# ScalarE copies the high parts of the exponentials, the state space outputs come one stage later, and the softmax sums are asked for later

## The chip, the cores and the metric

The kernel runs on one core of a Trainium2 chip. The metric is the device time of one execution in microseconds (us). The core has five engines with a queue of instructions each: TensorE (PE in the profile; PEld is its weight load), VectorE (DVE), ScalarE (ACT), GpSimd (POOL) and SyncE (SP). The first four compute, and SP issues the DMAs. An instruction waits at the head of its queue until the semaphores that it names are reached, and everything behind it on that engine waits with it.

## The reference

One layer of a decoder trunk, sequence 1024, width 1024, in fp32: three causal mixers side by side (forgetting attention, an S5 state space, HGRN2), merged by gates, then cross attention and SwiGLU. The change touches the first two mixers.

```python
def fox_attention(q, k, v, log_f):        # 8 heads x 64
    c = jnp.cumsum(log_f, axis=1)
    ...
        s = jnp.einsum('bqhd,bkhd->bhqk', qi, k, preferred_element_type=jnp.float32) * scale
        s = s + ci[..., None] - c_keys
        s = jnp.where(k_pos[None, :] <= q_pos[:, None], s, -jnp.inf)
        p = jax.nn.softmax(s, axis=-1).astype(v.dtype)
        return jnp.einsum('bhqk,bkhd->bqhd', p, v)

def s5_mixer(u, a_re, a_im, b_re, b_im, c_re, c_im, d_skip, log_dt, w_glu, b_glu):   # 32 groups x 16
    ...
    _, _, h_r, h_i = lax.associative_scan(_complex_linear_combine, elems, axis=1)
    y = (jnp.einsum('bsgp,ghp->bsgh', h_r, c_re.astype(f32))
         - jnp.einsum('bsgp,ghp->bsgh', h_i, c_im.astype(f32)))
    y = y.reshape(bsz, seq, S5_W) + d_skip.astype(f32) * uf
    z = jax.nn.gelu(y)
    out = z * jax.nn.sigmoid(z @ w_glu.astype(f32) + b_glu.astype(f32))
    return out.astype(u.dtype)

def reference(x, mem, ...):
    h = rmsnorm(x, norm_mix[l])
    proj = h @ w_in[l]
    ...
    merged = (gates[:, :, 0] * (y_fox @ wb[:BRANCH_W])
              + gates[:, :, 1] * (y_s5 @ wb[BRANCH_W:2 * BRANCH_W])
              + gates[:, :, 2] * (y_hg @ wb[2 * BRANCH_W:]))
    x = x + merged @ w_out[l]
    x = x + cross_attention(rmsnorm(x, norm_x[l]), rmsnorm(mem, norm_mem[l]), ...)
    x = x + swiglu(rmsnorm(x, norm_ffn[l]), w_gate_up[l], w_down[l])
```

## The kernel before

An fp32 product is made of three matmuls. Every operand is split into a high part (a rounded copy) and a low part (the operand minus that copy), and high by high, low by high and high by low are accumulated in PSUM. So each weight and each activation passes through a copy and a subtraction before TensorE may use it. Matmuls are at most 128 x 512, one PSUM bank.

The program is written as generators that are mixed while it is recorded. `drive` steps the generator of the current stage, and `pump` puts pieces of the input projection between its steps. These fillers (tiles `pj`, from a fixed list of jobs) are counted by an account of TensorE time, `self.pe`. `later(us, fn)` asks for a piece of work at the first step at which that account has moved on by `us`. `ahead(n, fn)` records a piece with a higher priority, by n places: 60 for the state space stage, 60 for the splitting of weights, 20 for what `later` asked for, 10 for the attention. A scheduler then orders each engine's instructions by priority and by data dependences, which follow the order in which the code was recorded. Big tiles live in an arena of 50 slots; a slot is reused when its last reader is done.

**The state space stage** (`s5_main`, some 115 to 320 us of the span) treats 32 groups of channels in 8 blocks of four groups, o = 0 to 7. Each block passes four stages, one block behind the other:

- `s5_prep(o)`: 8 DMAs on SP (L1095) load the block's inputs into a tile `s5u`, and GpSimd makes the block's matrices `s5x`.
- `s5_prep2(o)`: VectorE makes the rotations `s5e`; TensorE makes `s5g` and `s5k`; ScalarE copies both out of PSUM; 8 DMAs on SP (L1163) lay the copy of `s5k` out as a block Toeplitz matrix `toep`.
- `s5_body(o)`: TensorE makes `s5d1`; VectorE multiplies it into `s5dd`, runs the scan, and makes the carried states `kcs`.
- `s5_out(o)`: TensorE makes `s5y` out of `toep` with the inputs and out of `kcs`, alternately for the four groups. VectorE and ScalarE apply the gelu in `s5u`, and 8 DMAs on SP (L1218) store it to `sz_d`.

There are two buffers of `toep` and two of `kcs`, taken in turn:

```python
self.toep, self.kcs = ([t[:, 512 * i:512 * i + 512].rearrange("p (g c) -> p g c", g=4) for i in range(2)]
...
tz = self.toep[o % 2]                                     # in s5_prep2(o)
for s in range(8):
    nc.sync.dma_start(out=tz[16 * s:16 * s + 16, :, 16 * s:128], in_=ktv[:, :, 0:128 - 16 * s])
...
self.mm(c, tz[:, g], U[:, g], True, False)                # in s5_out(o): reads toep, then kcs
self.mm(c, Z1[:, g].rearrange("p k h -> p (k h)"), kc[:, g], False, True)
```

**The attention stage** (`fox_main`, some 320 to 640 us) has 16 units, one for each head and each half of the queries. A unit steps over 4 or 8 blocks of 128 keys. At each, TensorE makes scores `st`, ScalarE their exponentials `pf`, and GpSimd copies these to the high part of `pt` (a 128 x 512 block, on the diagonal 384, 256 and 128 wide ones). VectorE subtracts for the low part, GpSimd adds `pf` into the running sum `facc`, and TensorE multiplies `pt` by the values two blocks later (`pv`). Between them stand the maxima of the next unit: TensorE makes `mx`, VectorE reduces it to `mc`, TensorE transposes that (`mt`). At a unit's end `fox_out` splits `facc` into `ah`, high part on ScalarE and low part on VectorE. After every second unit it asks by `later` for `sums`: four matmuls `sm` with `ah`.

The buffer number that ends a name in the orders below tells tiles apart. The inputs `s5u` of blocks 0 to 7 are 868, 932, 1052, 1183, 1376, 1598, 1784 and 1983.

Of the kernel before, what the change touches and what calls it, by code (L numbers as in the profile page):

```python
# [13 lines left out]
AF = mybir.ActivationFunctionType  # L14
ALU = mybir.AluOpType
# [32 lines left out]
S5_US = 4.5  # L48
S5_W = (1.0, 0.6, 1.0, 1.2)
FOX_AT = 8  # L50
S5_END = 1.5
S5_BEG = 1.75
AH_P = 0
# [134 lines left out]
class Trunk:  # L188
# [538 lines left out]
                out.append(piece(i, c))  # L727
        return out + [chain, rows]

    hi_pool = (0, 1, 2, 3)  # L730

    def fox_main(self):
        units = self.fox_units()
        pend = deque()
        pre = self.fox_pre(units[0])
        for i, f in enumerate(pre):
            f()
            yield FOX_P[i >= len(pre) - 3]

        def drain(n):  # L740
            while len(pend) > n:
                pend.popleft()()

        for ui, un in enumerate(units):
            p, half, h = un
            self.unit = ui
            pre = self.fox_pre(units[ui + 1]) if ui + 1 < len(units) else []
            nj = 4 * half + 4
            per = [[] for _ in range(nj)]
            if pre:  # L750
                body, tail = pre[:-2], pre[-2:]
                w = nj - PRE_END[half]
                per[0].append(body.pop(0))
                b = BUILD[half]
                for i, f in enumerate(body):
                    per[min(b + i * (w - b) // len(body), w - 1)].append(f)
                per[w - 1].append(tail[0])
                per[nj - 1].append(tail[1])
            acc = self.u("facc")[:, 0:512]
            st = {}  # L760
            pf = None
            for j in range(nj):
                q0 = max(0, 128 * j - 512 * half)
                ps = self.psm("st")
                diag = j >= 4 * half
                self.mm(ps[:, q0:512], self.k1[h][:, 128 * j:128 * j + 128], self.q1[h][:, q0:512], True, False)
                self.mm(ps[:, q0:512], self.k2[h][:, 128 * j:128 * j + 128], self.q2[h][:, q0:512], False, not diag)
                if diag:
                    self.mm(ps[:, q0:q0 + 128], self.ident_r, self.mkq_r, False, True)
                if j % 2 == 0:  # L770
                    pf = self.u("pf").rearrange("p (a b) -> p a b", a=2)
                pr = pf[:, j % 2, q0:512]
                self.act(pr, ps[:, q0:512], AF.Exp)
                pt = self.u("pt", F32R).rearrange("p (a b) -> p a b", a=2)
                if j % 4 in self.hi_pool:
                    self.ts(pt[:, 0, q0:512], pr, 1.0, 0.0, ALU.mult, ALU.add, self.nc.gpsimd)
                else:
                    self.act(pt[:, 0, q0:512], pr, AF.Copy)
                self.sub(pt[:, 1, q0:512], pr, pt.bitcast(F32)[:, 0, q0:512])
                if j == 0:  # L780
                    p0 = pr
                elif j == 1:
                    self.add(acc[:, q0:512], p0[:, q0:512], pr, self.nc.gpsimd)
                    if q0:
                        self.ts(acc[:, 0:q0], p0[:, 0:q0], 1.0, eng=self.nc.vector)
                else:
                    self.add(acc[:, q0:512], acc[:, q0:512], pr, self.nc.gpsimd)

                def pv(j=j, q0=q0, pt=pt, un=un, st=st, nj=nj, acc=acc):
                    p, half, h = un  # L790
                    if j == 0:
                        st["o"] = self.psm("pv")
                    for i in range(2):
                        self.mm(st["o"][:, q0:512], self.vst[j][:, 256 * p + 128 * h:256 * p + 128 * h + 128], pt[:, i, q0:512],
                                start=j == 0 and i == 0, stop=j == nj - 1 and i == 1)
                    if j == nj - 1:
                        self.fox_out(un, st["o"], acc)
                pend.append(pv)
                drain(PV_LAG)
                for f in per[j]:  # L800
                    f()
                yield (0.5 + 0.5 * (512 - q0) / 512) * HALF_W[half] * (FOX_E[j - nj] if j >= nj - 2 else 1.0)
        while pend:
            yield 0.5
            drain(len(pend) - 1)
        yield

    def fox_out(self, un, o, acc):
        p, half, h = un
        b = 64 * h  # L810
        s, so = slice(b, b + 64), slice(64 - b, 128 - b)
        hs = slice(512 * half, 512 * half + 512)
        hd = 2 * p + h
        if half == 0 and h == 0:
            self.fy[p] = self.u(f"fy{p}")
        t = self.u("ft")
        self.act(t[s, 0:512], o[so], AF.Copy)
        self.add(self.fy[p][s, hs], o[s], t[s, 0:512])
        ah = self.u("ah", F32R).rearrange("p (a b) -> p a b", a=2)
        self.split(acc, ah[:, 0], ah[:, 1])  # L820

        self.fah.append((hd, ah))

        def sums():
            ps = self.psm("sm")
            todo, self.fah = self.fah, []
            for n, (hd_, a_) in enumerate(todo):
                for i in range(2):
                    self.mm(ps[0:8], self.ohc_r[:, hd_, 0:8], a_[:, i], start=n + i == 0,
                            stop=n == len(todo) - 1 and i == 1)  # L830
            if p == 0:
                self.nc.vector.tensor_copy(out=self.fsum[0:8, hs], in_=ps[0:8])
            else:
                self.add(self.fsum[0:8, hs], self.fsum[0:8, hs], ps[0:8])
        if h == 1:
            self.later(2.0, sums)
        if half == 1 and h == 1:
            self.nc.sync.dma_start(out=self.fy_d[p], in_=self.fy[p])

# [381 lines left out]
    def s5_main(self):  # L1221

        self.s5o = {}
        for o in range(11):
            for lag, stage in ((0, self.s5_prep), (3, self.s5_out), (1, self.s5_prep2), (2, self.s5_body)):
                if 0 <= o - lag < 8:
                    stage(o - lag)
                    yield S5_W[lag] * (S5_END if o > 8 else S5_BEG if o < 2 else 1.0)
            if o == FOX_AT:
                self.need("ff")  # L1230
                self.fox_alloc()
# [958 lines left out]
```

## Time and profile before

| | us |
|---|---|
| median of three runs | 2177.76 |
| the three runs | 2176.45, 2177.76, 2184.1 |
| the profiled execution, its own time | 2179.96 |
| its span in the trace | 2177.9 |
| PE busy in the span | 2105.1 |
| DVE, ACT, POOL busy | 1438.1, 775.3, 437.0 |

The profiled execution's time is 2.2 us above the median, and its span covers all but 2.1 us of it. Times in the trace count from the span's start. A wait of an engine is its idle time just before an instruction, put down to the event that came last. A matmul's duration overlaps that of the next one, so the time that a row of matmuls takes is read from the distance of their starts.

### The profile page before, as it was taken

Reading aid. Unit: us, or ns where it says so; the run is one execution under the profiler, and the core shown is the slowest. Engines: PE = TensorE matmul, PEld = TensorE weight load, DVE = VectorE, ACT = ScalarE, POOL = GpSimd, SP = SyncE. Lnnn points to the kernel's source line nnn. Section 1 sums busy time; section 2 is a strip of 40 time slices with the busy share of each in tenths; the row PEclk is TensorE's granted clock in tenths of the full one; section 3 lists DMA queues with packets and bytes.
Section 4 is the critical chain, followed back from the end, with each engine's and each line's share of the span. In section 5 each row is a group of like instructions: output and inputs, shape, how many; then the busy total and the mean of one; then the engine's idle time right before and its main releaser. Section 6 shows DMA issues by size and latency. Waiting matters only on the chain.

```text
span 2177.9 us, 26388 instructions
## 1 busy us (share of the span) xinstructions
PE 2105.1 (97%) x10176; PEld 1728.0 (79%) x10176; DVE 1438.1 (66%) x2193; ACT 775.3 (36%) x1208; POOL 437.0 (20%) x399
## 2 busy tenths in 40 slices
PE   7998999999999999999999999998899999999999
PEld 5887776677788888888888888786688888878887
DVE  8887898889745566537665677665877777753421
ACT  4113255555421322227244455433433333331210
POOL 4271204454531111002411000011211111100000
PEclk9999999999999999999999999999999999999999
DMA  4432220111211011125434434142222222172311
GB/s 162 138 99 71 51 84 20 49 48 31 68 63 41 28 68 54 64 107 194 154 107 154 147 107 145 65 154 92 87 87 81 74 78 87 68 277 79 122 55 57
DMA packets 74925, 202.40 MB, mean 93 GB/s; under 512 B 13352, under 2 KB 23080, under 8 KB 74800
## 3 DMA queue, kind: packets, MB, share of 16 engines
q1 hardware_dynamic: 74800, 200.72, 26.7%
q8 instruction: 80, 1.31, 0.2%
q14 instruction: 45, 0.37, 0.1%
HBM read 156.51 MB, written 42.99 MB: 92 GB/s over the span
## 4 chain that ended last, share of the span: by engine, by line
PE 67%; DVE 3%; ACT 1%; issue 1%; DMA 1%; POOL 0%; SPq 0%; POOLq 0%; DVEq 0%; ACTq 0%
PE pj L221 43%; PE fp L221 18%; PE hs L221 2%; PE xo L221 1%; PE rs L221 1%; PE xs L221 1%; PE ho L221 1%; PE hst L221 0%; DVE xr L251 0%; DMA xr<-x_d 0%; PE pv L221 0%; POOL t L239 0%; PE st L221 0%; PE fb L221 0%; DVE wl L239 0%
## 5 line engine op out<-in xcount | busy, mean ns | idle before, releaser
L221 PE MATMUL pj<-xh,wh 128*128 128x512 f32 x784 | 312.2, 403 | 7.2 <-ACT xh L236 5.8
L221 PE MATMUL pj<-xl,wh 128*128 128x512 f32 x784 | 314.1, 404 | 4.8 <-DVE xl L251 4.8
L221 PE MATMUL pj<-xh,wl 128*128 128x512 f32 x784 | 310.2, 399 | 0.0
L239 DVE TENSOR_TENSOR wl<-wr,wh 128x1024 fp32r<-128x1024 f32 (+3 forms) x162 | 193.2, 1194 | 51.0 <-ACT wh L236 49.0
L221 PE MATMUL fp<-th,wc 128*128 128x512 f32 x640 | 206.8, 389 | 0.0
L236 ACT ACTIVATE wh<-wr 128x1024 fp32r<-128x1024 f32 (+3 forms) x162 | 155.0, 960 | 144.2 <-PE pj L221 58.0
L221 PE MATMUL fp<-fx,wc 128*128 128x512 f32 x720 | 175.0, 392 | 7.5 <-ACT wc L236 7.3
L221 PEld LDWEIGHTS pj<-xh,wh 128*128 128x128 f32 x784 | 148.4, 189 | 39.8 <-ACT xh L236 6.3
L239 DVE TENSOR_TENSOR xr<-pj,xr 128x512 f32<-128x512 f32 x80 | 54.8, 689 | 186.5 <-PE pj L221 177.2
L221 PEld LDWEIGHTS pj<-xl,wh 128*128 128x128 f32 x784 | 147.9, 189 | 36.7 <-DVE xl L251 7.1
L221 PEld LDWEIGHTS pj<-xh,wl 128*128 128x128 f32 x784 | 148.3, 189 | 30.6 <-issue 2.2
L221 PEld LDWEIGHTS fp<-fx,wc 128*128 128x128 f32 x720 | 136.1, 189 | 36.8 <-ACT wc L236 7.8
L221 PEld LDWEIGHTS fp<-th,wc 128*128 128x128 f32 x640 | 120.1, 188 | 25.0
L221 PE MATMUL pj<-hh,wh 128*128 128x512 f32 x352 | 133.9, 391 | 3.0 <-ACT hh L236 3.0
L221 PE MATMUL pj<-hh,wl 128*128 128x512 f32 x352 | 133.9, 391 | 1.4 <-DVE wl L239 1.4
L221 PE MATMUL pj<-hl,wh 128*128 128x512 f32 x352 | 134.2, 392 | 0.5 <-DVE hl L239 0.5
L221 PE MATMUL fp<-tl,wc 128*128 128x512 f32 x320 | 124.5, 389 | 0.0
L239 POOL TENSOR_TENSOR fc<-fc,fs 128x512 f32<-128x512 f32 x40 | 58.2, 1454 | 327.6 <-ACT fs L236 317.7
L239 DVE TENSOR_TENSOR pt<-pf,pt 128x512 fp32r<-128x512 f32 (+1 forms) x96 | 94.4, 985 | 40.1 <-POOL pt L255 39.8
L239 POOL TENSOR_TENSOR acc<-acc,sq 128x512 f32<-128x512 f32 (+1 forms) x18 | 30.7, 1707 | 375.4 <-ACT sq L236 375.3
L255 POOL TENSOR_SCALAR pt<-pf 128x512 fp32r<-128x512 f32 (+1 forms) x96 | 67.6, 705 | 139.1 <-ACT pf L236 127.8
L236 ACT ACTIVATE fs<-fc 128x512 f32<-128x512 f32 x40 | 25.3, 632 | 154.7 <-DVE fc L239 154.7
(415 smaller groups left out, 4758.9 us busy)
## 6 DMA issues: line engine op xcount, KB each, us to landing
wr<-w_in SPq DMA_DIRECT2D x48, 512.0 KB, 4.2
wr<-w_gu SPq DMA_DIRECT2D x44, 512.0 KB, 3.8
h_d<-fc SPq DMA_DIRECT2D x22, 512.0 KB, 2.6
hr<-h_d SPq DMA_DIRECT2D x22, 512.0 KB, 6.0
gz_d<-gz SPq DMA_DIRECT2D x20, 512.0 KB, 2.9
gate<-gz_d SPq DMA_DIRECT2D x20, 512.0 KB, 3.4
wr<-xo SPq DMA_DIRECT2D x17, 512.0 KB, 4.9
xr<-x_d SPq DMA_DIRECT2D x16, 512.0 KB, 6.2
```

Source lines behind the costliest of these rows:

```text
L221: self.nc.tensor.matmul(out, lhsT, rhs, start=start, stop=stop)
L236: self.nc.scalar.activation(out=out, in_=in_, func=f, **kw)
L239: return (eng or self.nc.vector).tensor_tensor(out=out, in0=a, in1=b, op=op)
L255: (eng or self.nc.vector).tensor_scalar(out=out, in0=a, scalar1=s1, scalar2=s2, op0=op0, **kw)
```

## The change

Three edits:

- in `fox_main` the high part of all 96 blocks of `pt` is copied by ScalarE (an ACTIVATE with Copy) in place of GpSimd;
- in `s5_main` the stages of one round o are recorded as prep(o), prep2(o-1), out(o-3), body(o-2); before, out(o-3) stood ahead of prep2(o-1);
- in `fox_out` the sums are asked for 6.0 us of TensorE's account later, in place of 2.0.

```diff
+SUM_AT = 6.0
...
-    hi_pool = (0, 1, 2, 3)
...
-                if j % 4 in self.hi_pool:
-                    self.ts(pt[:, 0, q0:512], pr, 1.0, 0.0, ALU.mult, ALU.add, self.nc.gpsimd)
-                else:
-                    self.act(pt[:, 0, q0:512], pr, AF.Copy)
+                self.act(pt[:, 0, q0:512], pr, AF.Copy)
                 self.sub(pt[:, 1, q0:512], pr, pt.bitcast(F32)[:, 0, q0:512])
...
         if h == 1:
-            self.later(2.0, sums)
+            self.later(SUM_AT, sums)
...
         for o in range(11):
-            for lag, stage in ((0, self.s5_prep), (3, self.s5_out), (1, self.s5_prep2), (2, self.s5_body)):
+            for lag, stage in ((0, self.s5_prep), (1, self.s5_prep2), (3, self.s5_out), (2, self.s5_body)):
```

Blocks b and b+2 share a buffer of `toep`. With the new order of the code, the copies of block b+2 into that buffer are recorded ahead of the reads of block b, for b = 0 to 5. So these six blocks read the matrix of the block two further on, which changes this part of the computation, and their first read depends on the eight copies of block b+2. The buffers of `kcs` are not crossed in this way.

What moves is shown at three places. The line numbers of the changed kernel are one higher in the helpers and four lower in the state space code.

**TensorE at the output of block 1.** `s5y` with `s5u_932` is block 1's output, `s5g` and `s5k` with `s5x_1192` are block 3's matrices, `s5d1_1545` belongs to block 2, and `pj` are filler matmuls. Before:

```order
L221 MATMUL pj_1412<-xh0_78,wh_1256 128x512
L221 MATMUL s5y_1419<-s5u_932,toep_823 128x128
L221 MATMUL pj_1412<-xl0_86,wh_1256 128x512
...
L221 MATMUL s5y_1419<-kcs_824,s5x_941 128x128
...
L221 MATMUL pj_1476<-wh_1365,xh0_78 128x512
L226 MATMUL s5g_1503<-cst_76,s5x_1192 128x128 x4
L221 MATMUL s5k_1508<-s5cx_643,s5x_1192 16x16
L221 MATMUL s5k_1508<-s5x_1192 16x112
...
L221 MATMUL s5d1_1545<-s5u_1052,s5x_1061 128x128 x4
```

After:

```order
L227 MATMUL s5g_1427<-cst_76,s5x_1192 128x128 x4
L222 MATMUL s5k_1432<-s5cx_643,s5x_1192 16x16
L222 MATMUL s5k_1432<-s5x_1192 16x112
...
L222 MATMUL pj_1412<-xl0_86,wh_1262 128x512
...
L222 MATMUL pj_1412<-xh7_85,wl_1263 128x512
L222 MATMUL s5y_1463<-s5u_932,toep_823 128x128
L222 MATMUL s5y_1463<-kcs_824,s5x_941 128x128
...
L222 MATMUL s5d1_1545<-s5u_1052,s5x_1061 128x128 x4
```

Block 3's matrices moved ahead of block 1's output; between the last `s5k` and the first `s5y` stand 23 filler matmuls.

**SP around the copies of blocks 5 and 6.** `toep_823<-s5u_1598` are the copies of block 5 (the last of the eight stands here), `toep_823<-s5u_1784` those of block 6. `sz_d` with `s5u_1183` and `s5u_1376` are the stores of blocks 3 and 4; `s5u_1983` are the loads of block 7; `wr` is a raw weight. Before:

```order
L1218 DMA sz_d_72<-s5u_1183 16x4x128 x8
L1163 DMA toep_823<-s5u_1598 16x512
...
L1163 DMA toep_823<-s5u_1598 16x4x16
L341 DMA wr_1970<-w_in 128x1024
L1095 DMA s5u_1983<-su_d_69 16x4x128 x8
L341 DMA wr_2074<-w_in 128x1024
L1163 DMA toep_823<-s5u_1784 16x512
L1218 DMA sz_d_72<-s5u_1376 16x4x128 x8
```

After:

```order
L1159 DMA toep_823<-s5u_1598 16x512
...
L1159 DMA toep_823<-s5u_1598 16x4x16
L1214 DMA sz_d_72<-s5u_1183 16x4x128 x8
L342 DMA wr_1970<-w_in 128x1024
L1091 DMA s5u_1983<-su_d_69 16x4x128 x8
L1159 DMA toep_823<-s5u_1784 16x512
L1159 DMA toep_823<-s5u_1784 16x4x112
```

The stores of an output moved behind the copies of the block two further on, and the copies of block 6 still stand behind the loads of block 7.

**TensorE at the sums after a pair of units, in the middle of the attention.** `sm` are the sums with two units' `ah`, `pv_4301` is the last output of the unit that ends there, `st_4405` and (after) `st_4411`, `pv_4391`, `mx` belong to the next. Before:

```order
L221 MATMUL pv_4301<-pt_4331,vs_1754 128x128
L221 MATMUL pj_4284<-xh5_83,wh_3996 128x512
...
L221 MATMUL pj_4284<-xh7_85,wl_3997 128x512
L221 MATMUL pj_4392<-xh0_78,wh_3996 128x512
L221 MATMUL sm_4399<-ah_4252,crr_170 8x512 x2
L221 MATMUL sm_4399<-ah_4379,crr_170 8x512
L221 MATMUL st_4405<-q12a_2350,k10_2346 128x512
```

After:

```order
L222 MATMUL st_4411<-q12a_2344,k10_2340 128x512
...
L222 MATMUL pv_4391<-pt_4364,vs_1619 128x512
...
L222 MATMUL mx_4424<-k21_2343,qmm_2346 128x128
L222 MATMUL mx_4424<-crr_170 128x128
L222 MATMUL mx_4428<-k21_2343,qmm_2346 128x512
L222 MATMUL sm_4431<-ah_4246,crr_170 8x512 x2
L222 MATMUL sm_4431<-ah_4373,crr_170 8x512 x2
L222 MATMUL st_4443<-q12a_2344,k10_2340 128x512
```

The sums moved behind a block of the next unit's scores, outputs and maxima.

## Rows read from the trace of the kernel before

**Rows 1.** The page's first part: busy time of each engine in us, its share of the span, and its instructions.

```profile
PE 2105.1 (97%) x10176; PEld 1728.0 (79%) x10176; DVE 1438.1 (66%) x2193; ACT 775.3 (36%) x1208; POOL 437.0 (20%) x399
```

**Rows 2.** Windows of 50 us, one in the state space stage and one in the attention: start and end; length; busy time of PE, PEld, DVE, ACT and POOL with their instructions; granted clock of TensorE, share of the DMA engines, GB/s.

```profile
200.00:250.00 50.00, 45.93 (x222) 38.02 (x220) 41.36 (x75) 12.03 (x24) 11.75 (x10) 0.93 0.16 38
500.00:550.00 50.00, 45.96 (x207) 35.53 (x206) 44.83 (x64) 26.78 (x45) 26.01 (x30) 0.97 0.07 22
```

**Rows 3.** Waits of TensorE from 150 to 620 us: engine, tile and line that waited, what released it; us in total, times, the longest.

```profile
PE s5y L221 <- DVE kcs L239: 10.1, 6, 3.3
PE sm L221 <- DVE ah L239: 8.0, 5, 2.3
PE mt L226 <- DVE mc L239: 7.9, 9, 1.7
PE pj L221 <- DVE wl L239: 1.5, 2, 0.9
PE st L221 <- ACT q12a L236: 1.4, 3, 0.6
...
PE sm L221 <- ACT ah L236: 0.4, 1, 0.4
```

**Rows 4.** The same windows as in group 2, 4 us long, around two waits of the state space stage and one of the attention.

```profile
168.00:172.00 4.00, 2.72 (x12) 2.72 (x13) 1.79 (x3) 0.00 (x0) 0.00 (x0) 0.65 0.42 156
172.00:176.00 4.00, 4.00 (x19) 3.37 (x19) 2.24 (x6) 0.95 (x2) 0.00 (x0) 0.92 0.00 0
...
208.00:212.00 4.00, 4.00 (x17) 3.81 (x17) 2.33 (x8) 0.00 (x0) 0.00 (x0) 0.50 0.03 5
212.00:216.00 4.00, 4.00 (x15) 3.16 (x15) 4.00 (x8) 2.55 (x3) 0.00 (x0) 0.80 0.16 31
...
512.00:516.00 4.00, 3.14 (x10) 2.51 (x11) 2.63 (x5) 1.12 (x2) 1.24 (x2) 0.74 0.00 0
516.00:520.00 4.00, 4.00 (x17) 3.31 (x17) 3.53 (x5) 1.03 (x2) 2.49 (x3) 0.83 0.41 110
```

**Rows 5.** Timeline of TensorE at these waits and at the places that the change moves: start, duration, engine, line, operation, tile and shape, number of instructions, idle time before the first and its releaser.

```profile
169.28 0.80 PE L221 MATMUL s5y<-kcs,s5x 128*128 128x128 f32 x2 [2.61 <-DVE kcs L239]
...
207.67 0.80 PE L221 MATMUL s5y<-kcs,s5x 128*128 128x128 f32 x2 [3.33 <-DVE kcs L239]
...
213.94 0.40 PE L221 MATMUL pj<-wh,xl 128*128 128x512 f32 x1
214.17 0.40 PE L221 MATMUL pj<-wl,xh 128*128 128x512 f32 x1
...
234.55 1.05 PE L221 MATMUL s5d<-s5u,s5x 128*128 128x128 f32 x8
...
256.57 0.35 PE L221 MATMUL s5k<-s5x 128*16 128x112 f32 x2
...
356.29 0.40 PE L221 MATMUL sm<-ah,crr 128*8 128x512 f32 x1 [1.78 <-DVE ah L239]
...
512.86 0.40 PE L221 MATMUL sm<-ah,crr 128*8 128x512 f32 x1 [2.29 <-DVE ah L239]
```

**Rows 6.** Timeline of ScalarE: the copy that follows that `s5k`.

```profile
257.60 0.57 ACT L236 ACTIVATE s5u<-s5k 16x512 f32<-16x512 f32 x1
```

**Rows 7.** Timeline of SP's queue: eight issues each of the `toep` copies, of the stores of an output and of the loads of a block, with the time from the first to the end of the last.

```profile
181.35 5.05 SPq L1163 DMA_DIRECT2D toep<-s5u  x8
...
217.96 3.59 SPq L1218 DMA_DIRECT2D sz_d<-s5u  x8
224.55 4.80 SPq L1095 DMA_DIRECT2D s5u<-su_d  x8
```

**Rows 8.** The view of one tile, `toep`: from issue to landing.

```profile
DMA to landing us min/median/max: 1.7/1.9/2.7
```

**Rows 9.** Timeline of VectorE: the work around block 1's and block 2's outputs (`z` is a filler's evacuation, `negc` ends a chain of the forget gates, `wl` is a weight's low part, `s5u` the gelu), and the end of block 4's body.

```profile
177.08 0.69 DVE L239 TENSOR_TENSOR z<-pj,Rb 128x512 f32<-128x512 f32 x1
...
184.88 2.29 DVE L531 TENSOR_TENSOR_SCAN negc<-on,a 128x1024 f32<-128x1024 f32 x1
187.88 1.23 DVE L239 TENSOR_TENSOR wl<-wr,wh 128x1024 fp32r<-128x1024 f32 x1 [0.72 <-ACT wh L236]
...
211.06 1.12 DVE L251 SCALAR_TENSOR_TENSOR s5u<-s5u,s5rv,s5y 128x128 f32<-128x128 f32 x4 [1.67 <-PE s5y L221]
...
217.25 0.68 DVE L239 TENSOR_TENSOR s5u<-s5u 128x512 f32<-128x512 f32 x1
...
246.45 1.38 DVE L239 TENSOR_TENSOR s5dd<-s5dd,s5e 64x508 f32<-64x508 f32 x2
```

**Rows 10.** Groups of instructions from 330 to 620 us by line, engine, operation, tile and shape: count; busy time, mean ns of one; idle time of the engine before them and what ended it.

```profile
L239 DVE TENSOR_TENSOR pt<-pf,pt 128x512 fp32r<-128x512 f32 x47 | 61.0, 1301 | 30.7 <-POOL pt L255 30.5
L255 POOL TENSOR_SCALAR pt<-pf 128x512 fp32r<-128x512 f32 x47 | 34.8, 744 | 62.7 <-ACT pf L236 56.9 <-DVE pt L239 2.3 <-DVE ah L239 2.2
L239 POOL TENSOR_TENSOR facc<-facc,pf 128x512 f32<-128x512 f32 x24 | 34.7, 1446 | 4.6 <-ACT pf L236 4.6
L236 ACT ACTIVATE pf<-st 128x512 f32<-128x512 f32 x47 | 27.8, 597 | 48.5 <-PE st L221 40.0 <-DVE pt L239 6.0 <-DVE fy L239 1.4
...
L239 DVE TENSOR_TENSOR ah<-facc,ah 128x512 fp32r<-128x512 f32 x15 | 11.1, 742 | 0.2
L236 ACT ACTIVATE ah<-facc 128x512 fp32r<-128x512 f32 x15 | 9.4, 625 | 0.6 <-DVE pt L239 0.5
```

## The prediction

> **What bounds the kernel now.** I read the page's first part, then windows over the two stages that the change touches, then TensorE's waits there, and last the timelines around the longest of them. TensorE is busy 97% of the span [rows 1], so only its idle time and its slow clock can be won or lost here; its work stays the same. From 150 to 620 us it waits for few things [rows 3]: `s5y` for `kcs` 10.1 us, `sm` for `ah` 8.0 and 0.4, `mt` for `mc` 7.9, a weight's low part 1.5, ScalarE's `q12a` 1.4. In all of them but the last and the 0.4 VectorE is late. It is busy 41.4 of 50 us in the state space stage and 44.8 of 50 in the attention, where ScalarE has 26.8 and GpSimd 26.0 [rows 2].
>
> A long wait costs a second time. After the waits of 2.61 and 3.33 us at 169.28 and 207.67, and after that of 2.29 at 512.86 [rows 5], the mean granted clock of the next windows is 0.65 and 0.92, 0.50 and 0.80, 0.74 and 0.83 [rows 4]: matmuls ran partly at 1.2 GHz. The loss is one minus the clock, times 4 us: 1.7, 2.8 and 1.7 us. The wait of 1.78 at 356.29 is followed by matmuls 0.40 long and close together, so I count no loss there.
>
> **Part 1, the outputs one stage later.** What it removes: all of the 10.1 us, if VectorE has finished `kcs` by the later place, and with it 1.7 + 2.8 us of clock. With the 1.5 for weights, which lies on the same chains, the stage now loses 16.1 us.
>
> What it adds is a dependence. The first `s5y` matmul of block b now waits for the eight copies of block b+2 into the same `toep` buffer, and those come late by their nature: they begin with block b+2's `s5k`, which now stands right ahead of it. From the end of `s5k` (256.57 + 0.35) to the end of ScalarE's copy (257.60 + 0.57) it is 1.25 us [rows 5, 6]. Eight issues take 5.05 us of SP's queue, the last starting some 4.4 us in [rows 7], and a copy lands 1.9 us after issue [rows 8]: 7.55 us. The cover is filler matmuls, 0.23 us apart [rows 5]. By the order after, 23 of them, 5.3 us, stand in it for blocks 1, 2, 4 and 5, and about 10.6 us for blocks 0 and 3. So four waits of at least 2.3 us follow, 9.2 us, each as long as one that lost clock before. Behind the waiting `s5y` on TensorE stand fillers, the next block's `s5d1` and the next `s5g`; VectorE's gelu and the slot of the inputs wait in turn.
>
> What SP has in front of the copies comes on top. Block 1: the copies of block 3 stand behind eight stores and four of the eight loads that came free late; I estimate 3.5 us. Block 2: the copies of block 4 stand behind the stores of block 1's output and the loads of block 6. That output's gelu runs on VectorE after the forget gates' chain. From 177.77 (end of `z`) to 187.17 (end of `negc`) it is 9.4 us, then two weight parts of 1.2, the evacuation 1.1, some 6 us of work in between (from 211.06 to 217.93 before it is 6.9 with the evacuation) [rows 9], eight stores 3.6 and eight loads 4.8 [rows 7], and copies and landing 6.3: 33 us. TensorE has 90 matmul rows, 20.4 us, between the outputs of blocks 1 and 2. That is a loss of 12.5 us with the clock after block 1, or 6.5 if the 6 us in between is overlapped; I take 9. Block 4: the loads of block 7 wait for a slot until block 4's body is done. From its `s5d1` at 234.55 [rows 5] to the end of `s5dd` at 247.83 [rows 9] it is 13.3 us, with 2.9 of block 3's gelu put ahead 16.2; then loads 4.6 and copies 6.3: 27 us against 18.5 of TensorE's rows, a loss of 8.5. Block 5: 1 us, since the copies of block 7 start while TensorE stands at block 4. Left of the waits for `kcs`, at the last two blocks, 2 us. Slow clock after blocks 2 and 4 as after 207.67, 2.8 each.
>
> Sum: 3.5 + 9 + 2.8 + 8.5 + 2.8 + 1 + 2 = 29.6, against 16.1: **+13 us**. Low end: every wait at its floor of 2.3 us, no clock lost, 2 us for `kcs`: 11.2 - 16.1 = -5. High end: 12.5 in place of 9, and blocks 0 and 3 waiting 2.3 each: 37.7 - 16.1 = +21.
>
> **Part 2, the sums later.** The four matmuls of a sum wait for the low part of `ah`, 8.4 us over six waits, the longest 2.29 [rows 3, 5]. By the order, 2.2 to 3.9 us of matmul time stood between a unit's last `pv` and the last `sm` matmul; now 5.5 to 11.3. Needed is at most 3.9 + 2.3 = 6.2, so the waits go nearly all, and the 1.7 us of clock after 512.86 with them: **-10**. What is late next is `mt`, since VectorE is as busy as before. The sums hold a PSUM buffer no longer than before, and the tile `ah` some 4 us longer.
>
> **Part 3, the copies on ScalarE.** GpSimd loses 96 copies, 47 of the wide ones 744 ns each [rows 10]. ScalarE gains them, 128x512 fp32r out of fp32 in SBUF, the same form as `ah<-facc` on ScalarE, 625 ns [rows 10]: 48 x 0.625 = 30 us for the wide ones, and between 0 and 30 for the narrower ones; I estimate 18 by their widths. That is 48 us in some 320 us of attention, about 7.5 in 50, so ScalarE goes from 26.8 to about 34 of 50 [rows 2]. The cover is its idle time: ahead of the wide exponentials alone it waited 48.5 us, 40.0 of it for TensorE's scores [rows 10]. Exponential and copy of one block take 0.60 + 0.63 = 1.2 us, well under the pace of some 3.3 us for each of the 96 blocks in 320 us. Where that cover fails, ScalarE's `q12a` comes later: 1.4 us of waits now, I take +1, between 0 and +4 (three times as many).
>
> VectorE's subtraction waited 30.5 us for GpSimd's copy [rows 10], and that turns into a wait for ScalarE's, about as long: 0.63 in place of 0.74. The question is the subtraction itself, 1301 ns beside 742 for `ah<-facc,ah` in the same form [rows 10]. If it fell to 742, 47 x 0.56 = 26 us of VectorE would be free, and I price that at 6 of the 7.9 us of `mt`; if it stays, 0. I take **-2**, nearer to the second, since the add into `facc` (1446 ns) still follows each exponential and runs beside the subtraction.
>
> The Trainium skill (SBUF — State Buffer, section "SBUF: two separate sides") speaks against a gain here: a VectorE instruction with two SBUF inputs and a GpSimd instruction that reads SBUF share a port pair as a lock, and the one that comes second waits for the whole instruction of the other. The 1301 beside 742 agrees with it. By that rule the add, which can now start at the end of the exponential while ScalarE copies, stands in the subtraction's way as before, and the term would be 0, so the sum +4 in place of +2; by a fall to 742 it would be -2.
>
> Attention together: -10 - 2 + 1 = **-11**, from -16 (-10 - 6) to -4 (+4 for ScalarE, and 2 us of sum waits left).
>
> **Sum.** +13 - 11 = +2 us. Against the profiled span of 2177.9 that is 2180. The profiled execution's own time is 2.2 us over the median; against the median 2177.76 it is 2180 as well. I forecast **2180**. A measurement of this kernel can tell about 0.5%, 11 us, from no change: faster is below 2167, slower above 2189.
>
> **Rivals.**
> A, faster. The copies of `toep` are never behind other transfers, because VectorE, no longer late for `kcs`, runs earlier through the gelu and so the stores and loads are issued earlier. Then the waits stand at their floor, without loss of clock (-5), and the attention gains near its best (-15): 2178 - 20 = 2158; with the 1.7 us of clock that followed a wait of 2.29 behind each of the four, 2165. For it: the waits for `kcs` are all of one cause, and the floor is only 2.3 us. Against it: SP's order is fixed, with stores and loads ahead of the copies of blocks 4 and 7, and their tiles depend on VectorE, 83% busy.
>
> B, slower. The copies are held at blocks 2 and 4 as worked out, with nothing overlapped and blocks 0 and 3 reached too (+21), and the attention gains less than planned, as ScalarE holds up `q12` (-8): 2178 + 13 = 2191. It decides where the copies' last landing comes over 10 us behind the cover at one of the two blocks.
>
> C, the sums' waits only move: VectorE is the late engine in the attention, and PE, reaching `mt` 8 us sooner over the stage, waits there instead. The attention gives -3, and with +13 it is 2188.
>
> **How the numbers follow.** The forecast has 0.45, A 0.25, B 0.20, C 0.10. A lies under 2167 at both its ends. B lies above 2189; C lies at the bound, and I put 0.04 of it above. So faster 0.25, same 0.51, slower 0.24. The forecast alone reaches from 2170 to 2188. Over all cases, a range from 2159 to 2193 leaves out about a tenth at each side: nearly half of A's chance under it, and nearly half of B's above.
>
> **What would show it.** Part 1: the row `s5y` waiting for `kcs` shrinks to about 2 us, and in its place stand waits of `s5y` for DMAs of `toep`, four or more, the longest at blocks 2 and 4, with a granted clock of about 0.5 in the windows behind. If these waits are absent, or all near 2.3, A holds. Part 2: `sm` for `ah` gone; if `mt` for `mc` grows by as much, C holds. Part 3: GpSimd's `pt` rows gone and ScalarE's there at about 625 ns; the mean of VectorE's subtraction tells whether it fell from 1301 and by how much; a long `st` for `q12` shows ScalarE late. The forecast is wrong if the clock doesn't fall behind the new waits, or if SP's stores and loads are issued before VectorE's chains as I put them.

## The result: 0.6% slower

| | before | changed |
|---|---|---|
| median, us (5 runs each) | 2179.28 | 2192.69 |
| ratio, 95% interval | | 1.0058 [1.0045, 1.0072] |
| span of the profiled execution, us | 2177.9 | 2192.6 |

The loss is 12.6 us by the ratio and 14.7 us between the two profiled spans. The page's first part after the change, as [rows 1]:

```profile
PE 2110.8 (96%) x10176; PEld 1733.7 (79%) x10176; DVE 1424.1 (65%) x2193; ACT 823.1 (38%) x1305; POOL 382.9 (17%) x303
```

TensorE did the same work in 5.7 us more of busy time, which is slow clock, and stood idle 9.0 us longer (81.8 against 72.8, span less busy). Where the idle time lies is read from TensorE's waits, 150 to 640 us, as [rows 3]:

```profile
PE s5y L222 <- DMA toep<-s5u: 20.9, 4, 7.5
PE mt L227 <- DVE mc L240: 4.4, 5, 1.2
PE pv L222 <- DVE pt L240: 2.5, 5, 0.7
PE st L222 <- ACT q12a L237: 2.0, 4, 0.6
PE st L222 <- ACT q12b L237: 1.9, 2, 1.2
PE rs L222 <- ACT sq L237: 1.8, 1, 1.8
PE s5y L222 <- DVE kcs L240: 1.8, 2, 1.1
PE sm L222 <- DVE ah L240: 1.2, 1, 1.2
```

The waits for `kcs` went from 10.1 to 1.8 us, and 20.9 us of waits for the `toep` copies stand in their place. The sums' waits went from 8.4 to 1.2 us, and the small waits for `pt`, `q12` and `sq` grew. The four new waits in TensorE's timeline, against those of [rows 5]:

```profile
179.83 0.76 PE L222 MATMUL s5y<-s5u,toep 128*128 128x128 f32 x2 [6.12 <-DMA toep<-s5u]
...
207.69 0.77 PE L222 MATMUL s5y<-s5u,toep 128*128 128x128 f32 x2 [5.14 <-DMA toep<-s5u]
...
263.91 0.77 PE L222 MATMUL s5y<-s5u,toep 128*128 128x128 f32 x2 [7.50 <-DMA toep<-s5u]
...
285.62 0.70 PE L222 MATMUL s5y<-s5u,toep 128*128 128x128 f32 x2 [2.10 <-DMA toep<-s5u]
```

These are blocks 1, 2, 4 and 5. What makes one 7.50 and another 2.10 shows where ScalarE's copy and SP's issues are set side by side, for blocks 4 and 5; ScalarE first, then SP:

```profile
252.53 0.57 ACT L237 ACTIVATE s5u<-s5k 16x512 f32<-16x512 f32 x1
...
278.62 0.57 ACT L237 ACTIVATE s5u<-s5k 16x512 f32<-16x512 f32 x1
```

```profile
253.80 3.62 SPq L1091 DMA_DIRECT2D s5u<-su_d  x8
257.52 5.05 SPq L1159 DMA_DIRECT2D toep<-s5u  x8
...
279.21 5.05 SPq L1159 DMA_DIRECT2D toep<-s5u  x8
```

For block 5 SP issues at 279.21, the moment the copy ends (278.62 + 0.57), and the wait is 2.10: the floor. For block 4 the copy ends at 253.10, but SP is at the loads of block 7 until 257.42 and issues the first copy at 257.52: 4.4 us more.

To compare whole stages, I sum TensorE's idle time and its clock loss (one minus the granted clock, times its busy time) over windows of 2 us, 100 to 330 us for the state space, 330 to 660 for the attention, and all else in the span. Each sum is of one execution. The 59 executions of the kernel before that were run beside the experiments took from 2174.6 to 2186.1 us, all under 2178 at a mean granted clock of 0.993 or more and all over 2184 at 0.989, so the idle part of a sum is firmer than its clock part. Changes against the kernel before, us:

| | state space | attention | the rest | span |
|---|---|---|---|---|
| before, total | 15.9 | 21.1 | 48.7 | 2177.9 |
| changed, total | 30.1 | 15.1 | 55.2 | 2192.6 |
| difference | +14.2 | -6.0 | +6.5 | +14.7 |

### The profile page after: what moved, and what is told of

Its sections match the earlier page's. It is cut to its first block, busy times and chain, and to the rows that moved or that the text cites. A ratio compares the mean times of both kernels' runs of the same rounds, so it can differ in the third digit from the quotient of the medians.

```text
span 2192.6 us, 26442 instructions
## 1 busy us (share of the span) xinstructions
PE 2110.8 (96%) x10176; PEld 1733.7 (79%) x10176; DVE 1424.1 (65%) x2193; ACT 823.1 (38%) x1305; POOL 382.9 (17%) x303
## 4 chain that ended last, share of the span: by engine, by line
PE 68%; DVE 3%; ACT 1%; issue 1%; DMA 1%; POOL 0%; SPq 0%; POOLq 0%; DVEq 0%; ACTq 0%
PE pj L222 43%; PE fp L222 17%; PE hs L222 2%; PE xo L222 1%; PE rs L222 1%; PE xs L222 1%; PE ho L222 1%; PE pv L222 0%; PE st L222 0%; PE hst L222 0%; DVE xr L252 0%; DMA xr<-x_d 0%; POOL t L240 0%; PE fb L222 0%; DVE wl L240 0%
## 5 line engine op out<-in xcount | busy, mean ns | idle before, releaser
L240 DVE TENSOR_TENSOR pt<-pf,pt 128x512 fp32r<-128x512 f32 (+1 forms) x96 | 71.6, 750 | 40.5 <-ACT pt L237 40.4
L240 POOL TENSOR_TENSOR facc<-facc,pf 128x256 f32<-128x256 f32 (+1 forms) x64 | 72.9, 1140 | 121.0 <-ACT pf L237 109.0
L237 ACT ACTIVATE fs<-fc 128x512 f32<-128x512 f32 x40 | 25.3, 632 | 154.4 <-DVE fc L240 154.4
```

What stands on the lines that cost most here:

```text
L237: self.nc.scalar.activation(out=out, in_=in_, func=f, **kw)
L240: return (eng or self.nc.vector).tensor_tensor(out=out, in0=a, in1=b, op=op)
```

## The experiments

Ratios are against the kernel before on the same chip, from 5 to 12 executions of each run. The last two columns are the sums just described, in us, from each run's one trace. Two traces are far from their run's median: e1's execution was the shortest of its twelve (2171.86, median 2177.29), e6's the longest of its six (2195.06, median 2188.03).

| run | ratio, 95% interval | state space | attention |
|---|---|---|---|
| e1_copies | 0.9990 [0.9978, 1.0002] | 14.8 | 14.9 |
| e2_order | 1.0113 [1.0098, 1.0128] | 29.8 | 26.6 |
| e3_sums | 1.0044 [1.0028, 1.0060] | 15.0 | 23.3 |
| e4_copies_sums | 1.0009 [0.9998, 1.0020] | 14.7 | 21.0 |
| e5_four_toep | 1.0080 [1.0067, 1.0093] | 29.9 | 18.8 |
| e6_order_copies | 1.0052 [1.0040, 1.0064] | 31.7 | 13.8 |
| e7_toep_act | 1.0051 [1.0039, 1.0063] | 23.7 | 15.0 |
| e8_four_toep_sums2 | 1.0051 [1.0039, 1.0063] | 28.7 | 15.4 |
| e9_body_first | 1.0030 [1.0018, 1.0043] | 25.3 | 14.4 |
| e10_matrices_early | 1.0077 [1.0058, 1.0096] | 28.1 | 18.3 |
| e11_rotations_early | 1.0045 [1.0028, 1.0063] | 26.6 | 16.0 |
| e12_low_pool | 1.0020 [1.0008, 1.0033] | 15.7 | 19.4 |

### The three edits one at a time

**The copies alone** (on the kernel before):

```diff
-    hi_pool = (0, 1, 2, 3)
+    hi_pool = ()
```

> The kernel before with the high parts copied by ScalarE and nothing else. Theory (the loss of the whole change lies in the state space stage, the attention gains about 6 us): of the attention's terms this one alone brings the shorter subtraction (waits of mt 7.9 to about 4.5, minus 3.5 us) and costs the new waits seen after the change, pv for the low part of pt (+2.5) and q12 on ScalarE (+2): +1 us, between -2 and +3, 2180. Rival 1 (ScalarE's copies are what makes the change slow): +6 us or more. Rival 2 (the faster subtraction is worth more than the sums' place): -5 us or less, since the sums' waits of 8.4 us shrink as well.

Measured: -0.1%, which can't be told from none. In its trace the attention loses 6.2 us less than before, 4.5 of it idle time; the trace is the fastest execution, so how much of the 6.2 the others keep isn't shown. The waits of the sums are halved although the sums stand where they stood:

```profile
PE mt L226 <- DVE mc L239: 7.0, 7, 1.6
PE sm L221 <- DVE ah L239: 2.6, 5, 1.0
PE st L221 <- ACT q12a L236: 2.2, 3, 0.9
PE sm L221 <- ACT ah L236: 1.6, 3, 1.0
```

Rival 1 is out. Rival 2 names the right mechanism (the sums' waits fell), though the time confirms at most half of it.

**The order alone:**

```diff
-            for lag, stage in ((0, self.s5_prep), (3, self.s5_out), (1, self.s5_prep2), (2, self.s5_body)):
+            for lag, stage in ((0, self.s5_prep), (1, self.s5_prep2), (3, self.s5_out), (2, self.s5_body)):
```

> The kernel before with the state space outputs one stage later and nothing else; as in the whole change, blocks 0 to 5 read the matrix of the block two further on. Theory: this holds the whole loss, waits for the toep copies of about 21 us in place of 10 for kcs, and 7 us more of slow clock: +17 to +20 us, about 2198, slower than the whole change. Rival (the loss is shared with the copies on ScalarE): +8 to +13 us, no slower than the whole change.

Measured: +1.13%, 24.6 us, twice the whole change's loss and above the theory's 17 to 20. The waits for `toep` came as the theory said, 20.8 us, and the state space part is as in the whole change (29.8 against 30.1). But the attention, in which nothing was edited here, lost 5.5 us more than before as well. The fillers fall in other places there (727 `pj` matmuls from 330 to 660 us, against 781 before); that this is the reason isn't shown.

**The later sums alone:**

```diff
-            self.later(2.0, sums)
+            self.later(6.0, sums)
```

> The kernel before with the sums asked for 6.0 in place of 2.0 later and nothing else. Theory: sm for ah falls from 8.4 us to about 1 and the slow clock after 512 us goes: -7 us, between -9 and -4, about 2172. Rival (the waits only move, since VectorE stays the late engine): -2 us or less of a gain, with mt for mc longer by 5 us or more.

Measured: +0.44%, slower. The theory fell, and the rival was still too mild; its sign, a longer `mt`, didn't come either (6.3 us against 7.9). The waits of `sm` did fall to 0.9 us. TensorE's longest from 330 to 660 us are now these:

```profile
PE mt L226 <- DVE mc L239: 6.3, 7, 2.4
PE pv L221 <- DVE pt L239: 4.3, 6, 1.4
PE mx L221 <- DVE pmx L702: 3.2, 1, 3.2
```

The longest of them, at 445.56, is TensorE waiting to write the maxima of the next unit while VectorE is still at other work. VectorE's timeline ahead of it has one gap, of 0.43 us:

```profile
436.82 0.75 DVE L251 SCALAR_TENSOR_TENSOR sq<-rs,cst,sq 128x512 f32<-128x512 f32 x1 [0.43 <-ACT sq L236]
...
441.60 1.76 DVE L239 TENSOR_TENSOR pt<-pf,pt 128x512 fp32r<-128x512 f32 x1
443.29 1.62 DVE L251 SCALAR_TENSOR_TENSOR qs<-qs,gq,ry 128x1024 f32<-128x1024 f32 x1
444.83 1.47 DVE L702 TENSOR_REDUCE pmx<-mx 128x1 f32<-128x512 f32 x3
```

In this trace, whose span is 7.2 us longer than before, the attention accounts for only 2.2 us of the loss. Another 4.2 lie outside both stages, 3.7 of them clock.

**Copies and sums, the order of before** (on the whole change):

```diff
-            for lag, stage in ((0, self.s5_prep), (1, self.s5_prep2), (3, self.s5_out), (2, self.s5_body)):
+            for lag, stage in ((0, self.s5_prep), (3, self.s5_out), (1, self.s5_prep2), (2, self.s5_body)):
```

> The whole change with the state space stages in the order of before: copies on ScalarE and later sums. Theory: the attention's part of the change by itself, -4 us of waits and -1.7 of clock as between the two traces: -4 to -8 us, about 2173, and the state space stage as before. Rival (the attention gained only because the state space stage had shifted the work around it): within 2 us of the kernel before.

Measured: +0.09%, the rival's result. The copies win the attention 2.3 us over e3, and the sums lose 6.1 against e1, 4.8 of them clock. The rival's reason doesn't hold for the copies: e1 had this order too, and its attention lost 14.9.

### Is it the dependence on the copies?

**Four `toep` buffers**, so that nothing is crossed:

```diff
-        tz, kz = self.u("toep"), self.u("kcs")
+        tz, kz, tz2 = self.u("toep"), self.u("kcs"), self.u("toep")
...
+        G.memset(tz2, 0.0)
...
+        self.toep = self.toep + more
...
-        tz = self.toep[o % 2]
+        tz = self.toep[o % 4]
```

> The whole change with four toep buffers (block o takes buffer o modulo 4) in a second tile, so that no output reads the matrix of the block two further on and none waits for its copies; the order of the code stays that of the change. Theory (the dependence is the loss of the state space stage): the 20.9 us of waits for toep go with the slow clock behind them, at most 4 us of waits for kcs are left there, and the span falls by 20 to 27 us: 2166 to 2173, below the kernel before. Rival (the order itself is bad, since VectorE's and SP's work comes later): waits for kcs or for the loads take their place, and no more than 8 us of the change's time is won back: 2185 or more.

Measured: +0.80%. The theory fell: the waits for `toep` are gone, and the stage loses as much as with them. TensorE's waits, 100 to 330 us:

```profile
PE s5y L222 <- DVE kcs L240: 13.1, 4, 5.5
PE rs L222 <- ACT sq L237: 4.9, 1, 4.9
PE s5k L222 <- POOL s5x L240: 1.7, 1, 1.7
```

Freed of the copies, the first `s5y` matmul moved ahead in TensorE's order again (block 2's ran at 183.11, and the next one, which needs `kcs`, at 205.29), so the waits for `kcs` came back. One way in which VectorE got late shows in ScalarE's and then VectorE's timeline:

```profile
269.63 0.60 ACT L237 ACTIVATE s5x<-s5g 128x512 f32<-128x512 f32 x1 [4.03 <-PE s5k L222]
270.13 0.57 ACT L237 ACTIVATE s5u<-s5k 16x512 f32<-16x512 f32 x1
270.61 1.04 ACT L237 ACTIVATE wh<-wr 128x1024 fp32r<-128x1024 f32 x1
```

```profile
271.68 1.23 DVE L240 TENSOR_TENSOR wl<-wr,wh 128x1024 fp32r<-128x1024 f32 x1 [4.93 <-ACT wh L237]
```

ScalarE's queue has the copy of `s5g` ahead of a weight, waits 4.03 us for TensorE, and VectorE waits 4.93 us for that weight.

**The same, sums asked for as before:**

```diff
-SUM_AT = 6.0
+SUM_AT = 2.0
```

> The whole change with four toep buffers and the sums asked for 2.0 later: only the copies on ScalarE and the order without its dependence. Theory: state space stage as in the run with four buffers, attention as in the run with the copies alone: 2160 to 2170, and within 4 us of the run with four buffers and later sums. Rival (the sums' place decides by how it falls together with VectorE's work, which shifts with every change ahead of it): more than 6 us from the run with four buffers, to either side.

Measured: +0.51%, 6.3 us under e5. The two stages' losses are as the theory said, near e5's in the state space and near e1's in the attention; its time is out, as e5's was, and so is "within 4 us" of e5. The rival's "more than 6" holds, barely.

**The copies of `toep` on ScalarE's queue:**

```diff
-            nc.sync.dma_start(out=tz[16 * s:16 * s + 16, :, 16 * s:128], in_=ktv[:, :, 0:128 - 16 * s])
+            nc.scalar.dma_start(out=tz[16 * s:16 * s + 16, :, 16 * s:128], in_=ktv[:, :, 0:128 - 16 * s])
```

> The whole change with the eight toep copies of each block issued by ScalarE's queue in place of SP's; as in the whole change, blocks 0 to 5 read the matrix of the block two further on. Theory (of the 20.9 us of waits about 9 are the way from s5k to the landing and 11 the stores and loads that SP has in front): the waits of s5y for toep fall to 8 to 12 us, four of about 2.3, and the span by 9 to 15 us: 2178 to 2184. Rival (the copies are late by their data or in the DMA engines, not by SP's queue): the waits stay above 17 us and the time within 4 us of the whole change.

Measured: +0.51% beside the whole change's +0.58%, and the rival's result by both of its signs, the waits only just. TensorE's waits for `toep`:

```profile
PE s5y L222 <- DMA toep<-s5u: 17.2, 4, 7.0
```

They were 20.9 us in the whole change. The stage's loss fell from 30.1 to 23.7, its clock part from 7.0 to 4.6. At block 2 the wait fell from 5.14 to 1.10. At block 1 it rose from 6.12 to 6.96, although the first copy was issued 0.04 us after ScalarE's own ended: the longest way from issue to landing was now 6.1 us, where it had been 2.5. SP, free of the copies, issued two weights of 512 KB from 174.07 on, beside the last copies on ScalarE's queue; in the whole change these two weights followed the copies, at 178.36. From 174 to 180 us the DMA engines were 89% busy or more. So SP's queue accounts for part of the lateness (block 2), and the transfers themselves for another (block 1).

**Order and copies, sums as before** (the same line in the whole change):

> The whole change with the sums asked for 2.0 later, as before. Theory (after the first four runs: the later place is worth nothing, since each wait of the sums that goes comes back as a wait of pv and mx for VectorE): within 4 us of the whole change, 2189 to 2197, with sm for ah back at 4 to 8 us and fewer waits of pv. Rival (the prediction's: the later place saves the waits): slower than the whole change by 6 us or more, 2199.

Measured: +0.52% beside the whole change's +0.58%. In the time the theory holds, and the prediction's view doesn't. Its signs came only in part: `sm` for `ah` rose to 3.4 us, not to 4, and the waits of `pv` for `pt` stayed (2.4 against 2.5).

### Which half of the earlier prep2?

**Body ahead of prep2**, with the copies on ScalarE:

```diff
-            for lag, stage in ((0, self.s5_prep), (3, self.s5_out), (1, self.s5_prep2), (2, self.s5_body)):
+            for lag, stage in ((0, self.s5_prep), (3, self.s5_out), (2, self.s5_body), (1, self.s5_prep2)):
```

> Copies on ScalarE, sums asked for 2.0 later as before, and a new order of the state space stages: prep(o), out(o-3), body(o-2), prep2(o-1), so that the body which makes kcs is recorded ahead of the next block's rotations and matrices. Two toep buffers, nothing crossed. Theory (now: what stands in VectorE's and ScalarE's queues ahead of kcs sets the wait of s5y; moving prep2 ahead of out was wrong, moving it behind body is right): waits of s5y for kcs fall from 10.1 to 6 us or less, the stage's idle time and slow clock from 15 to about 10, and the time is 3 to 8 us under the run with the copies alone: about 2171. Rival (the scheduler puts VectorE's work in the order of readiness, and the order of the code hardly matters there): kcs stays near 10 and the time within 3 us of the copies alone, about 2177; or body then waits for rotations that come later, and it is slower.

Measured: +0.30%, slower, where the theory had a gain. The waits for `kcs` fell as it said, from 10.1 to 3.2 us, and yet the stage lost 25.3 us, against 14.8 in e1: 4.2 more of idle time, 6.3 more of clock. TensorE's waits, 100 to 330 us:

```profile
PE rs L222 <- ACT sq L237: 7.4, 3, 3.7
PE s5y L222 <- DVE kcs L240: 3.2, 2, 2.4
PE mx L222 <- DVE qmm L668: 3.1, 1, 3.1
PE s5k L222 <- DVE s5u L252: 1.6, 1, 1.6
```

**Matrices early, rotations late** (on e5), and **rotations early, matrices late** (on the whole change). `s5_rot` is the part of prep2 with VectorE's rotations, `s5_mat` the rest; between the late half and the body no fillers are put:

```diff
-            for lag, stage in ((0, self.s5_prep), (1, self.s5_prep2), (3, self.s5_out), (2, self.s5_body)):
+            for lag, stage in ((0, self.s5_prep), (1, self.s5_mat), (3, self.s5_out), (1.5, self.s5_rot), (2, self.s5_body)):
```

```diff
-            for lag, stage in ((0, self.s5_prep), (1, self.s5_prep2), (3, self.s5_out), (2, self.s5_body)):
+            for lag, stage in ((0, self.s5_prep), (1, self.s5_rot), (3, self.s5_out), (1.5, self.s5_mat), (2, self.s5_body)):
```

> The run with four toep buffers, with prep2 cut in two: the matrices (s5g, s5k, ScalarE's two copies, the toep copies) stay ahead of the output, VectorE's rotations go back behind it. It tells which half of the earlier prep2 costs. Theory A (ScalarE's queue: its copy of s5g stands there early, waits for TensorE, and the weights' high parts wait behind it): the stage's loss of idle time and clock stays near the 30 us of the run with four buffers, and ScalarE's waits for s5k stay at 10 us or more; about 2195. Theory B (VectorE: the rotations stand in front of the output's and the body's work): the loss falls to 20 us or less, about 2184.

> The other half: in the whole change VectorE's rotations stay ahead of the output, and the matrices with ScalarE's copies and the toep copies go back behind it, so two toep buffers are enough and nothing is crossed. Theory A (ScalarE's queue and the copies' dependence): the stage's loss falls from 30 us to 18 or less, near the 15 of the order of before, and the time to about 2182. Theory B (VectorE's rotations in front): it stays at 25 us or more, about 2192, with waits for kcs of 12 us or more.

Measured: +0.77% and +0.45%; the stage lost 28.1 and 26.6 us, 10 us or more above the order of before with either half. TensorE's waits for `kcs`, e10 and e11:

```profile
PE s5y L222 <- DVE kcs L240: 13.8, 6, 5.7
```

```profile
PE s5y L222 <- DVE kcs L240: 12.5, 6, 4.2
```

e10 agrees with A, e11 with B (its time, 2188.6, lies between the two), so neither A nor B alone is the cause. ScalarE's waits for `s5k` from 150 to 330 us were 17.8 us in e10 and 4.4 in e11, 2.6 before, so part of the loss comes nearly without them. Not all of it: of the 10.7 us that e11's stage loses more than before, 4.9 lie between 100 and 150 us, where ScalarE waited 10.0 us for `s5k`, 5.4 before.

### VectorE relieved

**GpSimd subtracts the low part of `ah`** (on e4):

```diff
-        self.split(acc, ah[:, 0], ah[:, 1])
+        self.split(acc, ah[:, 0], ah[:, 1], lo_eng=self.nc.gpsimd)
```

> Copies on ScalarE and later sums with the order of before, and the low part of ah subtracted by GpSimd in place of VectorE (16 subtractions of 0.84 us). Theory (the sums' waits went and came back as waits of pv, mx and mt because VectorE has no idle time there): relieving VectorE takes some 4 to 8 us of idle time and clock out of the attention's 21, about 2175, without waits of the sums. Rival (the new waits come from the sums' PSUM tile or place, not from VectorE's load, or GpSimd's subtraction blocks VectorE's): within 3 us of the run without this edit, 2182, or slower.

Measured: +0.20%, no better than e4's +0.09%, the rival's result; the attention lost 19.4 us against 21.0. GpSimd's subtractions took 1.39 us on average, not 0.84. The theory's time is out. That VectorE's work makes the moved waits stays shown only at the place in e3's timeline.

No run beat the kernel before beyond its interval; e1, the copies alone, came nearest.

## Why the prediction was right and wrong

The time, 2192.7, lies in the range of 2159 to 2193, 0.3 us inside its upper end, and the outcome is the one with the chance of 0.24. The forecast of +2 us missed by some 11: 5 in the attention, 1 in the state space stage, and 5 to 7 in stretches that had no term. That it lies inside is luck: about half of the miss comes from where the range allowed for nothing.

**Part 1 was right in size.** It put the stage's loss after the change at 29.6 us; the windows give 30.1. Waits for `toep` and `kcs`: 3.5, 7.3 (9 less 1.7 of clock), 8.5, 1 and 2, together 22.3, against 6.1, 5.1, 7.5, 2.1 and 1.8, together 22.7. Single terms were off by up to 2.6 us and cancelled, which is luck too; the longest waits stand at blocks 4 and 1, where 2 and 4 were forecast. Clock: 7.3 against 7.0, with 1.4 to 2.3 behind each of the four waits. The floor of 2.3 us shows at block 5, 2.10. Blocks 0 and 3 did not wait, as forecast. That SP's stores and loads come ahead of the copies, in the forecast as in rival B, shows in the timeline of block 4 for the loads.

But as a statement on the edit, "what it adds is a dependence" is not the whole cause. With the dependence taken away (e5, e8) the stage lost 29.9 and 28.7 us. The nine kernels with another order, the change among them, lost 23.7 to 31.7 us there, the five with the order of before 14.7 to 15.9. Idle time alone shows it: 16.0 to 23.4 us in the nine, 11.4 to 11.8 in the five. What is shown is that each of these orders costs 8 to 16 us more in this stage. The second `toep` tile of e5, e8 and e10 also takes a slot of the arena from the others, but e9 and e11 lost 25.3 and 26.6 us without it and without the dependence. Which queue carries the loss is open: the halves of prep2 each cost most of what the whole costs, and when one wait was cured others took its place.

**Part 2 failed.** The step was "so the waits go nearly all, and the 1.7 us of clock ... with them: -10". They went (8.4 to 1.2 us, and no clock was lost in the attention), but over half of that the copies alone do (8.4 to 4.2 in e1), and moving the sums won nothing: alone it cost +0.44%, with the copies it cost the attention 6.1 us (e1 to e4), and in the new order 1.3 (e6 to the change). The attention's idle time rose by 0.5 to 1.7 us in each of the four pairs; the rest is clock. That is rival C in kind, and worse in size. It expected the wait to reappear at `mt`; it came at `pv`, and in e3 and e4 at `mx`.

**Part 3 was mis-sized.** It was given -2 + 1. In the trace of the copies alone the attention's loss falls by 6.2 us, from e3 to e4 by 2.3, from e2 to e6 by 12.8; its idle time alone falls by 4.5, 3.7 and 8.1. VectorE's subtraction is the reason that can be read. After the change, 330 to 640 us, as [rows 10]:

```profile
L240 DVE TENSOR_TENSOR pt<-pf,pt 128x512 fp32r<-128x512 f32 x48 | 48.3, 1014 | 28.0 <-ACT pt L237 27.9
...
L240 POOL TENSOR_TENSOR facc<-facc,pf 128x512 f32<-128x512 f32 x24 | 36.8, 1531 | 41.9 <-ACT pf L237 41.5
...
L237 ACT ACTIVATE pt<-pf 128x512 fp32r<-128x512 f32 x48 | 29.8, 631 | 2.6 <-PE sm L222 1.1 <-DVE pt L240 0.2
```

It fell from 1301 to 1014 ns, half the way to 742, while I took "nearer to the second", no fall. In the two traces, 330 to 640 us, the wide subtractions during which GpSimd ran nothing took 0.70 us at most (8 of 47 before, 14 of 48 after); the others had a mean of 1.43 us before and 1.15 after. The Trainium skill (SBUF — State Buffer, section "SBUF: two separate sides") tells of a lock between a VectorE instruction with two SBUF inputs and a GpSimd instruction that reads SBUF; these numbers agree with it. That the remaining add would stand in the way as before was my use of the rule, and that was wrong. The ScalarE copies cost 631 ns (625 expected), and ScalarE's `q12` waits rose from 1.8 to 3.9, +2.1 for the +1 taken. Unpriced were `pv` waiting for `pt` and `fy` (+2.9) and `rs` (+1.3).

**No term** stood for the rest of the span, +6.5 us. Of this 4.7 is clock, 3.4 of it at one place, below. That it comes from the change isn't shown: over the fourteen traces the clock lost outside the two stages goes from 6.8 us, in the kernel before, to 15.9 in e7.

## What to carry to other kernels

Before an order of stages is changed, look which buffers go round by a counter: a write recorded ahead of the older reads turns into a wait for that write, and into other values. Curing that wait gave nothing back here: in a schedule where several engines are nearly full, a wait is worth only what the next late thing leaves of it, so price a moved wait by a run with that one edit. And the edit that took instructions from beside a full engine (the copies) helped in two pairs of runs and made no difference that can be told in the third, where the one that only asks for work later (the sums) hurt in three pairs and made none in the fourth.

## What the runs showed of the hardware

**The same instructions ran at either clock.** At 790 us, far from all edits, the changed kernel lost 3.4 us of clock, and no wait between 660 and 1400 us was over 0.7. In the windows before, TensorE was fully busy, with matmuls of 8 rows (`fb`) among the fillers. The same stretch of the kernel before had 1.00. After the change, windows of 2 us, as [rows 2]; 0.50 is 1.2 GHz throughout a window:

```profile
788.00:790.00 2.00, 2.00 (x6) 0.84 (x5) 2.00 (x3) 0.86 (x1) 0.00 (x0) 1.00 0.00 0
790.00:792.00 2.00, 2.00 (x10) 1.70 (x10) 0.72 (x2) 0.63 (x1) 0.52 (x1) 0.71 0.04 8
792.00:794.00 2.00, 2.00 (x12) 2.00 (x11) 0.00 (x0) 0.00 (x0) 1.04 (x1) 0.50 0.00 0
```

Over all the traces the losses came mostly in pieces of some 1.4 to 3.4 us each, and places that no edit touched (10 to 40, 790, 1420 to 1570 us) had one more or one less: 5.2 us at 1400 to 1600 before, 4.6 to 7.1 in the others. The last alone is up to 0.1% of the span.

**A longer wait lost no more clock.** After the wait of 7.50 us TensorE lost 2.3 us, after that of 3.33 before it lost 2.9, after 5.14 it lost 1.4. The windows behind the 7.50:

```profile
264.00:266.00 2.00, 2.00 (x10) 2.00 (x11) 0.13 (x1) 0.00 (x0) 0.00 (x0) 0.50 0.64 207
266.00:268.00 2.00, 2.00 (x10) 1.90 (x10) 0.30 (x2) 0.00 (x0) 0.00 (x0) 0.50 0.10 39
268.00:270.00 2.00, 2.00 (x6) 0.82 (x5) 0.82 (x4) 0.69 (x2) 0.00 (x0) 0.85 0.00 0
```

**A scan slowed beside GpSimd.** A block's four scans take 1.36 us in the kernel before at 244.10, where GpSimd is idle. In the changed kernel those at 192.70 took 5.14 while GpSimd made the matrices of a block. Two more such groups in these two traces ran beside GpSimd, at 141.40 and 201.18 before, with GpSimd at work for their first 0.9 and 1.0 us; they took 2.12 and 2.22. No run tested this by itself. VectorE, then GpSimd:

```profile
192.70 5.14 DVE L1179 TENSOR_TENSOR_SCAN s5dd<-s5rv,s5dd 128x128 f32<-128x128 f32 x4
```

```profile
192.19 1.51 POOL L240 TENSOR_TENSOR s5x<-s5pw,s5cx 128x512 f32<-128x512 f32 x1
193.66 1.41 POOL L240 TENSOR_TENSOR s5x<-s5x,s5tm 128x512 f32<-128x512 f32 x1
195.15 1.06 POOL L240 TENSOR_TENSOR s5tm<-s5pw,s5cx 128x512 f32<-128x512 f32 x1
196.28 1.27 POOL L240 TENSOR_TENSOR s5x<-s5x,s5tm 128x512 f32<-128x512 f32 x1
```
